# One level of Strassen's algorithm in the gate and up products of a transformer step on Trainium2

## The chip, the core and the metric

The kernel runs on one core of one Trainium2 chip, as one launch. The metric is the device time of the launch in microseconds (us). A core has the matrix engine TensorE (PE; its weight loads are shown apart as PEld), VectorE (DVE), ScalarE (ACT) and GpSimd (POOL), and a queue (SP) that issues the DMAs. Each engine works through its own list of instructions in order and waits for the others at semaphores. On-chip data lie in SBUF; PE writes its sums to PSUM, whose 2 KB rows by partition are called banks here.

## The reference, cut to what matters

The reference is one step of a two-layer diffusion backbone on 128 prompt tokens and 512 sample tokens, in float32. Each layer is a half-step SwiGLU network (FFN), a token mixing, and a second such FFN; the change is in the four FFNs.

```python
D_MODEL, D_FF, DEPTH, SEQ, DEC_SEQ = 1024, 2816, 2, 128, 512

def swiglu(h, w_gate, w_up, w_down):
    return (jax.nn.silu(h @ w_gate) * (h @ w_up)) @ w_down

def half_ffn(x, shift, scale, gate, w_gate, w_up, w_down, g, b):
    h = modulate(x, shift, scale)
    return post_norm(x, FFN_HALF * swiglu(h, w_gate, w_up, w_down), gate, g, b)
```

The nine shift, scale and gate vectors of a layer are silu(c) times a 1024 x 9216 matrix `w_ada`, once for the prompt and once for the sample. Layer 0 mixes by attention, layer 1 by a Fourier transform.

## The kernel before

Features lie on the partitions (eight tiles of 128, index k), and the 640 tokens on the free axis, in two parts of 256 and 384 columns (first FFN) or 254 and 386 (the other three). The 2816 hidden features are 22 blocks f of 128.

A float32 product is run as three products of the type float32r. Each operand is split into a high part `hi`, rounded to float32r, and the rest `lo`, and PE sums w_hi x_hi, w_hi x_lo and w_lo x_hi in one bank (`mm3`, L398). A split is a cast (ACT or DVE) and a subtraction (DVE or POOL). Every weight is read from memory once per launch and split once: `block` (L386) takes one raw tile of [128, 1024] and makes hi and lo of it, the cast and the subtraction as one instruction each.

An FFN (`ffn`, L822) goes through the f in six groups (`GROUPS`, L37). For one f it runs gate and up for both parts: 2 x 2 x 8 k x 3 = 96 products. `hidden` (L922) takes silu(gate) x up from PSUM and splits it into `hd`. After each group come the down products of its f, for both parts and eight output tiles o, and `add_out` (L546) adds each finished bank times the gate vector to `ya` on DVE, in one instruction for a part without prompt tokens and two for the part with them.

Beside that, the first three FFNs work through the `w_ada` matrix. `matvec` (L433) multiplies a loaded tile [128, 1024] with silu(c) and sums it along the free axis, on DVE, two instructions per tile for the two vectors (the trace calls them `junk<-raw,cond,bada`, each followed by a short read of the sum). These are 48, 32 and 48 tiles in the first, second and third FFN, and none in the fourth.

The order of each engine's instructions is fixed when the program is built. PE's products are emitted in line. The other engines' work is written as generators, and `tick` (L325) emits their next pieces up to `AHEAD` = 500 ns before PE's estimated time. Where a piece may go to DVE or POOL (`sums`, L186) or to ACT or DVE (`copies`, L196), `choose` (L297) gives it to the engine that is estimated to end first, DVE with a handicap of `SPARED` = 200 ns. So a wrong estimate changes the order, and an engine whose turn it is waits, with all that is queued behind it.

At the end of an FFN the last group's down sums are normalised (mean, variance, scale, split of the next input into `hh` and `hl`), which is DVE, POOL and ACT work on eight tiles of each part; the next FFN's first products need it.

Helper functions record every operation of an engine under one line: L134 for DVE, ACT and POOL, L359 for PE.

Of the kernel before, what the change touches and what calls it, by code (L numbers as in the profile page):

```python
# [36 lines left out]
GROUPS = ((0, 4), (4, 4), (8, 4), (12, 4), (16, 2), (18, 4))  # L37
# [6 lines left out]
# Of the scheduling below, in ns: how far ahead of TensorE's queue the other engines' pieces are emitted, what  # L44
# speaks against DVE where a piece can go elsewhere, and what counts as the same time.
# [9 lines left out]
def pieces(parts, t0, n):  # L55
    """Where the tokens t0 to t0 + n lie: (part, column, tokens before, tokens)."""
    out = []
    for half, runs in enumerate(parts):
        for c, t, m in runs:
            a, b = max(t, t0), min(t + m, t0 + n)  # L60
            if a < b:
                out.append((half, c + a - t, a - t0, b - a))
    return out


class Clock:
    """Estimates in ns: by tile, when it will be written (and by which engine) and when its slot is free."""

    def __init__(self):
        self.ready, self.used, self.free = {}, {}, {}  # L70


class Pool:
    """A pool of tiles that notes which tile follows which in a slot; since: when its memory is free at the earliest."""
# [15 lines left out]
    def used(self, name):  # L90
        """When the last tile of that name will be through."""
# [3 lines left out]
class Slots:  # L95
    """Tiles of one shape in a pool, taken and given back in any order."""
# [7 lines left out]
    def free(self, n):  # L104
        return len(self.rest) >= n

    def take(self, n=None):
        ts = []
        for _ in range(n or 1):
            used = lambda x: self.of[x][0].used(x)  # L110
            name = min(self.rest, key=used)
            self.rest.remove(name)
            pool, shape, dtype = self.of[name]
            ts.append(pool.tile(shape, dtype, name=name, bufs=1))
            self.names[ts[-1].tensor.name] = name
        return ts if n else ts[0]

# [5 lines left out]
class Queue:  # L123
    """An engine, with an estimate in ns of when it will be through what it has been given."""
# [12 lines left out]
    def cost(self, op, args, aps, kw):  # L137
# [12 lines left out]
    def after(self, x):  # L150
        """When tile x can be read."""
        if x.tensor.name not in self.clock.ready:
            return 0
        t, of = self.clock.ready[x.tensor.name]
        return t + ((125 if of == "v" else 0) if of == self.name else 250 if self.name == "t" else 200 if of == "t" else 130)

    def run(self, aps, outs, dur):
# [6 lines left out]
        for x in outs:  # L164
            c.ready[x.tensor.name] = self.t, self.name
        for x in (*aps, *outs):
            c.used[x.tensor.name] = max(c.used.get(x.tensor.name, 0), self.t + 200)


class Loads:  # L170
    """The DMA queue."""
# [4 lines left out]
    def dma_start(self, out, in_):  # L176
        c = self.clock
        self.issued = max(self.issued, c.free.pop(out.tensor.name, 0), c.ready.get(in_.tensor.name, (0, 0))[0]) + 50
        self.t = max(self.t, self.issued) + 4e-3 * int(np.prod(out.shape)) / 0.354
        c.ready[out.tensor.name] = self.t + 1800, "d"  # L180
        c.used[out.tensor.name] = max(c.used.get(out.tensor.name, 0), self.t + 1800)
        c.used[in_.tensor.name] = max(c.used.get(in_.tensor.name, 0), self.t + 1800)
# [1913 lines left out]
```

## Time and profile before

| | before |
|---|---|
| time, median of 3 runs | 2508.52 us (2504.37 to 2513.58) |
| span of the profiled execution | 2503.6 us |
| PE busy | 2413.5 us (96%) |
| DVE busy | 1595.8 us (64%) |
| ACT busy | 723.5 us (29%) |
| POOL busy | 641.9 us (26%) |
| DMA | 259.03 MB, mean 103 GB/s |

The span runs from the first to the last instruction of the core. No time of the profiled execution is shown but its span, which lies 4.9 us below the median of the timed runs. The first FFN's body (its groups of f, without its start and its last normalisation) lies at 112 to 365 us, the second's at 980 to 1235, the third's at 1458 to 1712, the fourth's at 2090 to 2345. In the page's 40 slices of 62.6 us each, the digit is the busy share, or for PEclk the granted clock, in tenths. A busy PE is the time from a product's start to its modelled end, and single products overlap, so their pace is read from the distance of starts, not from a product's own duration.

### The profile page before, as it was taken

The numbers are of one execution on the slowest core, as the hardware profiler recorded it, in microseconds if no ns is written. First come the engines' busy times: TensorE is split into PE (matmuls) and PEld (weight loads), VectorE is DVE, ScalarE is ACT, GpSimd is POOL, SyncE is SP. The second block draws the span as 40 slices with busy tenths as digits, with TensorE's granted clock in tenths as the row PEclk, the third lists the DMA queues.
The fourth block names the chain that finished last, engine by engine and source line by source line (L and its number), as shares of the span: only waits on it lengthen the run. The fifth ranks groups of instructions, "written<-read, shape, count | busy, mean of one in ns | idle before, by whom it ended". The sixth has DMA issues, their size and how long they took to land. (4 is left out here: it accounts for less than half of the span.)

```text
span 2503.6 us, 39511 instructions
## 1 busy us (share of the span) xinstructions
PE 2413.5 (96%) x15713; PEld 2314.1 (92%) x15713; DVE 1595.8 (64%) x3194; ACT 723.5 (29%) x1475; POOL 641.9 (26%) x499
## 2 busy tenths in 40 slices
PE   7999999989989999999999999999989989999997
PEld 7999999987577999999999999999976879999997
DVE  8867766677567686456566677676687963323346
ACT  3221212254666442112122322211234322221122
POOL 6312221242322152013112421100245522201112
PEclk8999999999899999999999999999999989999998
DMA  6535434140012225134240354443423213112121
GB/s 247 177 118 176 143 118 160 34 135 31 7 36 78 85 84 169 64 122 149 95 136 27 102 174 137 132 147 118 136 81 108 90 43 102 65 63 76 51 76 43
DMA packets 86025, 259.03 MB, mean 103 GB/s; under 512 B 13832, under 2 KB 26824, under 8 KB 85712
## 3 DMA queue, kind: packets, MB, share of 16 engines
q1 hardware_dynamic: 85840, 256.50, 31.0%
q8 instruction: 124, 2.03, 0.3%
q14 instruction: 61, 0.50, 0.1%
HBM read 248.84 MB, written 5.52 MB: 102 GB/s over the span
## 5 line engine op out<-in xcount | busy, mean ns | idle before, releaser
L359 PE MATMUL a<-hh,wu 128*128 128x254 f32 (+3 forms) x3840 | 855.1, 311 | 4.7 <-DVE hh L134 4.6
L359 PEld LDWEIGHTS a<-hh,wu 128*128 128x128 f32 x3840 | 653.4, 190 | 6.7 <-DVE hh L134 5.8
L359 PE MATMUL a<-hd,wd 128*128 128x254 f32 (+3 forms) x4224 | 629.1, 310 | 3.7 <-DVE ya L134 3.4
L359 PEld LDWEIGHTS a<-hd,wd 128*128 128x128 f32 x4224 | 624.2, 189 | 6.7 <-issue 3.7
L359 PE MATMUL a<-hl,wu 128*128 128x386 f32 (+3 forms) x1920 | 597.5, 311 | 3.0 <-POOL hl L134 1.6
L359 PE MATMUL a<-hh,w 128*128 128x254 f32 (+6 forms) x2240 | 504.2, 314 | 1.3 <-ACT hh L134 0.9
L134 DVE CUSTOM_DVE_ANT_0 junk<-raw,cond,bada 128x1024 bf16<-128x1024 f32 x256 | 379.0, 1481 | 12.3 <-DMA raw<-in_w_ada 7.8
L359 PEld LDWEIGHTS a<-hh,w 128*128 128x128 f32 (+1 forms) x2240 | 380.2, 191 | 7.1 <-issue 2.5
L359 PEld LDWEIGHTS a<-hl,wu 128*128 128x128 f32 x1920 | 364.9, 190 | 4.6 <-DVE hl L134 2.2
L134 DVE TENSOR_TENSOR tmp<-tmp,a 128x254 f32<-128x254 f32 (+3 forms) x176 | 85.5, 486 | 430.1 <-PE a L359 420.3
L359 PE MATMUL a<-hl,w 128*128 128x254 f32 (+4 forms) x1056 | 329.8, 312 | 3.0 <-POOL hl L134 2.0
L134 DVE SCALAR_TENSOR_TENSOR ya<-a,gate,ya 128x128 f32<-128x128 f32 (+3 forms) x576 | 226.7, 433 | 145.7 <-PE a L359 144.7
L134 POOL TENSOR_TENSOR wu<-raw,wu 128x1024 fp32r<-128x1024 f32 x55 | 150.4, 2744 | 633.0 <-ACT wu L134 617.0
L134 ACT CAST hd<-tmp 128x386 fp32r<-128x386 f32 (+3 forms) x163 | 75.5, 463 | 513.2 <-DVE tmp L134 513.0
L359 PEld LDWEIGHTS a<-hl,w 128*128 128x128 f32 (+1 forms) x1056 | 200.4, 190 | 6.4 <-POOL hl L134 2.8
L134 POOL TENSOR_TENSOR w<-raw,w 128x1024 fp32r<-128x1024 f32 (+3 forms) x49 | 106.9, 2189 | 357.9 <-ACT w L134 356.8
L134 ACT ACTIVATE tmp<-a 128x254 f32<-128x254 f32 (+3 forms) x176 | 76.8, 437 | 323.3 <-PE a L359 322.6
L134 ACT CAST wu<-raw 128x1024 fp32r<-128x1024 f32 x110 | 113.2, 1047 | 160.4 <-DMA raw<-in_w_gu 122.1
L134 ACT CAST wd<-raw 128x1024 fp32r<-128x1024 f32 x66 | 68.2, 1047 | 254.7 <-PE a L359 153.7
L134 DVE TENSOR_TENSOR hd<-tmp,hd 128x254 fp32r<-128x254 f32 (+3 forms) x152 | 89.3, 588 | 65.2 <-ACT hd L134 64.9
L134 POOL TENSOR_TENSOR wd<-raw,wd 128x1024 fp32r<-128x1024 f32 x22 | 60.4, 2749 | 193.7 <-ACT wd L134 150.8
L134 DVE TENSOR_TENSOR wd<-raw,wd 128x1024 fp32r<-128x1024 f32 x70 | 95.0, 1365 | 10.5 <-ACT wd L134 9.8
(438 smaller groups left out, 2575.8 us busy)
## 6 DMA issues: line engine op xcount, KB each, us to landing
raw<-in_w_gu SPq DMA_DIRECT2D x176, 512.0 KB, 3.7
raw<-in_w_ada SPq DMA_DIRECT2D x128, 512.0 KB, 3.8
raw<-in_w_dn SPq DMA_DIRECT2D x88, 512.0 KB, 3.6
raw<-in_w_fin SPq DMA_DIRECT2D x16, 520.0 KB, 3.8
wd<-in_w_ada SPq DMA_DIRECT2D x16, 512.0 KB, 7.5
raw<-in_w_ab SPq DMA_DIRECT2D x11, 512.0 KB, 3.7
raw<-in_w_abo SPq DMA_DIRECT2D x8, 512.0 KB, 4.3
raw<-in_w_fout SPq DMA_DIRECT2D x8, 512.0 KB, 3.6
```

Of the source, the lines that this page charges most:

```text
L134: return getattr(self.engine, op)(*args, **kw)
L359: pe.engine.matmul(out, w, x, **kw)
```

## The change

For f = 3 to 19 (4 to 19 in the first FFN) the gate and up products are seen as one product of 2 x 2 blocks: rows gate and up, inner index the even and the odd features, columns the first and the last 320 tokens. One level of Strassen's algorithm in Winograd's form takes seven block products in place of eight. Each is 4 k x 3 = 12 products of 320 columns, so such an f takes 84 products in place of 96. Of the 88 f of the four FFNs, 16 + 3 x 17 = 67 go this way. The plain f that are left are 0 to 2 (0 to 3 in the first FFN), 20 and 21.

What a Strassen f needs beside the products: `weights` forms S1 to S4 from the four raw blocks of [128, 512] (four sums), and `operand` splits A11, A22, S1, S2, A12, S3, S4 (seven casts and seven subtractions of 512 columns, in place of two of each of 1,024). Once per FFN `form` builds T1 to T4 from the input in four steps (16 sums of 320 columns and 16 splits). Of the block sums, U2 and U3 are used twice, so `snap` copies a bank to SBUF on ACT three times per f, and DVE adds from PSUM.

The groups become eight, of 3, 3, 3, 3, 3, 2, 2, 3 f (`FOURS` keeps the old ones in another place), so there are two more rounds of down sums per FFN. The down sums of a group now come after the first f of the next group, and a Strassen f's last two block products are held back (`pending`) until the next f has begun. The number of raw tiles goes from 3 to 4, and the estimates of DVE's and PE's instructions are altered.

```diff
-GROUPS = ((0, 4), (4, 4), (8, 4), (12, 4), (16, 2), (18, 4))
+THREES = ((0, 3), (3, 3), (6, 3), (9, 3), (12, 3), (15, 2), (17, 2), (19, 3))
+FOURS = ((0, 4), (4, 4), (8, 4), (12, 4), (16, 2), (18, 4))
+HALF = NT // 2
+EVENODD = (0, 2, 4, 6, 1, 3, 5, 7)
+PARTS = ("A11", "A22", "S1", "S2", "A12", "S3", "S4")
...
-            return (0.52 if twice else 1.04) * n + 68 + 62 * len(by)
+            return (0.52 if twice else 1.04) * n + 150 + 62 * len(by)
...
-    return {"v": 68 + 1.04 * n, "g": 150 + 2.1 * n}
+    return {"v": 150 + 1.04 * n, "g": 150 + 2.1 * n}
...
-        pe.run([w, x], [out], max(0.833 * size(w) * (2 if x.dtype == F32 else 1), (0.4167 * size(x) + 2.5) * (4 if x.dtype == F32 else 1)))
+        pe.run([w, x], [out], max(0.833 * size(w) * (2 if x.dtype == F32 else 1), (0.44 * size(x) + 7) * (4 if x.dtype == F32 else 1)))
...
+        plain = 4 if early else 3
+        fast = lambda f: plain <= f < FT - 2
...
+                if fast(f):
+                    units += [("s", 0, f)]
...
+            if g < last:
+                held = [("d", half, o, g) for half in (0, 1) for o in ([(0, 1, 2)] if half == 0 else [(0,), (1,), (2,)]) + [(o,) for o in range(3, KT)]]
...
+        def operand(f, part, src, known):
+            key = "s", f, part
+            yield None, lambda: may(key, 1, False)
+            eng = yield copies(src), src
+            yield None, lambda: may(key, 1, False)
+            tickets.popleft()
+            t = ops.take()
+            self.clock.cut(t, D // 2)
+            hi, lo = t[:, :D // 2], t[:, D // 2:]
+            copy(eng, hi, src)
+            eng = yield sums(D // 2), hi
+            eng.tensor_tensor(lo, src, hi.bitcast(F32), ALU.subtract)
+            wf[f, part] = hi, lo
+            known.add(part)
...
+        def weights(f):
+            raws, known, n = graw[f], set(), D // 2
+            halves = lambda t: (t[:, :n], t[:, n:])
+            put = lambda part, src: self.spawn(operand(f, part, src, known))
+            a11, a12 = halves(raws[0])
+            put("A11", a11)
+            yield None, lambda: 1 in raws
+            a21, a22 = halves(raws[1])
+            put("A22", a22)
+            s3, s2, s1, s4 = a21, a22, a11, a12
+            eng = yield sums(n), a21
+            eng.tensor_tensor(s3, a11, a21, ALU.subtract)
+            yield None, lambda: "A22" in known
+            eng = yield sums(n), s3
+            eng.tensor_tensor(s2, a22, s3, ALU.subtract)
+            yield None, lambda: "A11" in known
+            eng = yield sums(n), s2
+            eng.tensor_tensor(s1, s2, a11, ALU.add)
+            put("S1", s1)
+            put("S2", s2)
+            put("A12", a12)
+            yield None, lambda: "A12" in known
+            eng = yield sums(n), s2
+            eng.tensor_tensor(s4, a12, s2, ALU.subtract)
+            put("S3", s3)
+            put("S4", s4)
+            yield None, lambda: len(known) == 7
+            self.raws.give(raws[0], raws[1])
+            del graw[f]
...
+        def form(p):
+            n = HALF
+            yield None, lambda: all(h[half][k] is not None for half in range(2) for k in (2 * p, 2 * p + 1))
+            b11, b12, b21, b22 = (xs[p][:, n * k:n * k + n] for k in range(4))
+            if p + 1 < KT // 2:
+                self.spawn(form(p + 1))
+            yield None, lambda: self.tmps.free(3) and self.xt.free(1)
+            a, b = (t[:, :n] for t in self.tmps.take(2))
+            ts = [self.xt.take(dtype=F32R)]
+            self.clock.cut(ts[0], n, 2 * n, 3 * n)
+            def split(x, t, c):
+                hi, lo = t[:, c:c + n], t[:, c + n:c + 2 * n]
+                eng = yield copies(x), x
+                copy(eng, hi, x)
+                eng = yield sums(n), hi
+                eng.tensor_tensor(lo, x, hi.bitcast(F32), ALU.subtract)
+                return hi, lo
+            eng = yield sums(n), xs[p]
+            eng.tensor_tensor(a, b12, b11, ALU.subtract)
+            eng = yield sums(n), xs[p]
+            eng.tensor_tensor(b, b22, b12, ALU.subtract)
+            forms["T1", p] = yield from split(a, ts[0], 0)
+            eng = yield sums(n), b
+            eng.tensor_tensor(a, b, b11, ALU.add)
+            forms["T3", p] = yield from split(b, ts[0], 2 * n)
+            eng = yield sums(n), a
+            eng.tensor_tensor(b, b21, a, ALU.subtract)
+            self.xt.give(xs[p])
+            ts.append(self.xt.take(dtype=F32R))
+            self.clock.cut(ts[1], n, 2 * n, 3 * n)
+            forms["T2", p] = yield from split(a, ts[1], 0)
+            forms["T4", p] = yield from split(b, ts[1], 2 * n)
+            self.tmps.give(a, b)
+            formed.extend(ts)
...
+        def product(ps, f, part, xs, start):
+            self.need(lambda: (f, part) in wf)
+            w = wf.pop((f, part))
+            for k in range(KT // 2):
+                self.mm3(ps, [x[:, 128 * k:128 * k + 128] for x in w], xs(k), start and k == 0, k == KT // 2 - 1, not start)
+                if k == KT // 2 - 1:
+                    ops.give(w[0])
+                self.tick()
...
+        b11, b21, b22 = block_of(0, 0), block_of(1, 0), block_of(1, HALF)
+        t1, t2, t3, t4 = (formed_by(f"T{k}") for k in (1, 2, 3, 4))
...
+        def snap(st, name, ps):
+            yield "s", ps
+            yield "s", lambda: self.tmps.free(1)
+            st[name] = self.tmps.take()[:, :HALF]
+            nc.scalar.copy(st[name], ps)
...
+        def gate_a(f, st):
+            yield "v", st["b3"]
+            t = st["p1"]
+            yield "v", t
+            nc.vector.tensor_tensor(t, st["b3"], t, ALU.add)
+            self.banks.give(st["b3"])
+            yield "s", t
+            nc.scalar.activation(out=t, in_=t, func=AF.Silu)
+            yield "v", lambda: "up a" in st
+            yield "v", st["b1"]
+            nc.vector.tensor_tensor(t, t, st["b1"], ALU.mult)
+            self.banks.give(st["b1"])
+            yield from kept(f, "a", t, slice(0, HALF))
...
+        def up_b(st):
+            yield from snap(st, "u3", st["b1"])
+            st["u3 there"] = 1
+            t = st["u3"]
+            yield "v", t
+            nc.vector.tensor_tensor(t, st["b2"], t, ALU.add)
+            st["up b"] = 1
+        def gate_b(f, st):
+            yield "v", st["b2"]
+            t, up = st["u2"], st["u3"]
+            nc.vector.tensor_tensor(t, st["b2"], t, ALU.add)
+            self.banks.give(st["b2"])
+            yield "s", t
+            nc.scalar.activation(out=t, in_=t, func=AF.Silu)
+            eng = yield sums(HALF), t
+            eng.tensor_tensor(t, t, up, ALU.mult)
+            self.tmps.give(up)
+            yield from kept(f, "b", t, slice(HALF, NT))
...
+        def p4(f, st):
+            self.need(lambda: "u3 there" in st)
+            product(st["b1"], f, "A22", t4, False)
+            st["up a"] = 1
+        def p3(f, st):
+            self.need(lambda: "up b" in st)
+            product(st["b2"], f, "S4", b22, False)
+            self.spawn(gate_b(f, st), first=1)
...
+        def strassen(f):
+            st = {}
+            st["b1"] = self.take()[:, :HALF]
+            product(st["b1"], f, "A11", b11, True)
+            self.spawn(snap(st, "p1", st["b1"]), first=1)
+            st["b2"] = self.take()[:, :HALF]
+            product(st["b2"], f, "S1", t1, True)
+            flush(1)
+            self.need(lambda: "p1" in st)
+            product(st["b1"], f, "S2", t2, False)
+            self.spawn(snap(st, "u2", st["b1"]), first=1)
+            st["b3"] = self.take()[:, :HALF]
+            product(st["b3"], f, "A12", b21, True)
+            self.spawn(gate_a(f, st), first=1)
+            flush(1)
+            self.need(lambda: "u2" in st)
+            product(st["b1"], f, "S3", t3, False)
+            self.spawn(up_b(st), first=1)
+            pending.extend([(p4, f, st), (p3, f, st)])
...
-    g["w_gu"] = w.reshape(DEPTH, 2, 2, KT, 128, FT, 128).transpose(0, 1, 5, 2, 4, 3, 6).reshape(DEPTH, 2, FT, 2, 128, D)
+    g["w_gu"] = w.reshape(DEPTH, 2, 2, KT, 128, FT, 128)[:, :, :, EVENODD, :].transpose(0, 1, 5, 2, 4, 3, 6).reshape(DEPTH, 2, FT, 2, 128, D)
```

On DVE, in a group of the third FFN, this stood in the program before: two `w_ada` products, the splits of down weights (`wd`), and one f's hidden block (`mod` is the short read after a `w_ada` product):

```order
L134 ISA junk,mod_5_14177<-raw_15982,cond,bada 128x1024
L134 ISA mod_5_14177 128x1
L134 CAST wd<-raw_15986 128x1024
L134 TENSOR_TENSOR wd<-raw_15986,wd 128x1024
L134 TENSOR_TENSOR tmp_15998<-tmp_15998,a_15957 128x386
L134 CAST hd_5_16012<-tmp_15998 128x386
L134 TENSOR_TENSOR hd_4_16013<-tmp_15998,hd_5_16012 128x386
L134 TENSOR_TENSOR wd<-raw_15993,wd 128x1024
```

At a like place of the changed program stand the sums S1 to S4 made in place in the raw tiles, and the splits of their results into `wu` and `w`, ahead of two `w_ada` products:

```order
L183 TENSOR_TENSOR raw_16635<-raw_16635 128x512
L183 TENSOR_TENSOR raw_16633<-raw_16635,raw_16633 128x512
L183 CAST wu_16831<-raw_16635 128x512
L183 CAST w_16836<-raw_16633 128x512
L183 TENSOR_TENSOR wu_16829<-raw_16633,wu_16829 128x512
L183 TENSOR_TENSOR w_16836<-raw_16633,w_16836 128x512
L183 TENSOR_TENSOR wu_16851<-raw_16635,wu_16851 128x512
L183 ISA junk,mod_5_14549<-raw_16779,cond,bada 128x1024
L183 ISA mod_5_14549 128x1
L183 ISA junk,mod_5_14549<-raw_16779,cond,bada 128x1024
L183 ISA mod_5_14549 128x1
L183 TENSOR_TENSOR tmp_16824<-a_16861,tmp_16824 128x320
```

What moved in: the sums over halves of a raw tile, each waiting for the one before, stand ahead of the `w_ada` products and of the sum from PSUM (`tmp<-a,tmp`), which now all stand behind them in DVE's list.

On PE, at the same place, the program before went from one f's gate chain straight to its up chain, three products for each k:

```order
L359 MATMUL a_15957<-hh_7_14132,w 128x386
L359 MATMUL a_15957<-hl_7_14133,w 128x386
L359 MATMUL a_15957<-hh_7_14132,w 128x386
L359 MATMUL a_16008<-hh_0_14030,wu 128x386
L359 MATMUL a_16008<-hl_0_14031,wu 128x386
L359 MATMUL a_16008<-hh_0_14030,wu 128x386
```

Now the last k of A11 x B11 goes to one bank (`a_16804`), S1 x T1 (`xt` holds the T) to a second, and S2 x T2 is then added to the first bank:

```order
L433 MATMUL a_16804<-hh_84,w_16534 128x320
L433 MATMUL a_16804<-hl_92,w_16534 128x320
L433 MATMUL a_16804<-hh_84,w_16534 128x320
L433 MATMUL a_16820<-xt_14885,wu_16578 128x320 x3
L433 MATMUL a_16820<-xt_14912,wu_16578 128x320 x3
L433 MATMUL a_16820<-xt_14995,wu_16578 128x320 x3
L433 MATMUL a_16820<-xt_15066,wu_16578 128x320 x3
L433 MATMUL a_16804<-xt_14961,wu_16583 128x320 x3
```

What moved: between the two uses of the first bank stands ACT's copy of it (`snap`), so PE's list now waits on ACT within an f, and on each split of an operand 12 products ahead of its use, where it waited on one split for 48 products.

## Rows read from the trace of the kernel before

**Rows 1.** The page: its first line, PE's totals, the granted clock in 40 slices.

```profile
span 2503.6 us, 39511 instructions
PE 2413.5 (96%) x15713; PEld 2314.1 (92%) x15713; DVE 1595.8 (64%) x3194; ACT 723.5 (29%) x1475; POOL 641.9 (26%) x499
...
PEclk8999999999899999999999999999999989999998
```

**Rows 2.** Busy us (x instructions), clock, DMA by stretch; columns named first.

```profile
core 0: us, PE busy (x) PEld busy (x) DVE busy (x) ACT busy (x) POOL busy (x), PEclk, DMA share, GB/s
112.00:365.00 253.00, 253.00 (x1728) 253.00 (x1728) 175.18 (x264) 51.34 (x78) 57.61 (x21) 1.00 0.41 138
1458.00:1712.00 254.00, 254.00 (x1726) 254.00 (x1725) 181.43 (x289) 52.38 (x77) 36.89 (x14) 1.00 0.45 148
2090.00:2345.00 255.00, 255.00 (x1736) 255.00 (x1734) 80.78 (x149) 51.10 (x76) 36.16 (x13) 1.00 0.22 72
...
1847.00:2090.00 243.00, 212.96 (x1183) 185.51 (x1182) 178.25 (x423) 86.00 (x212) 112.59 (x97) 0.91 0.29 95
...
1373.00:1458.00 85.00, 81.80 (x528) 81.07 (x529) 62.15 (x116) 31.07 (x59) 41.75 (x35) 0.98 0.32 107
```

**Rows 3.** Timeline of PE in the second FFN: start us, us, instruction.

```profile
1300.35 0.34 PE L359 MATMUL a<-hl,wu 128*128 128x386 f32 x1
...
1300.88 0.34 PE L359 MATMUL a<-hl,wu 128*128 128x386 f32 x1
```

**Rows 4.** Third FFN, 1458 to 1712: groups on DVE; count, busy us, mean ns, idle before.

```profile
L134 DVE CUSTOM_DVE_ANT_0 junk<-raw,cond,bada 128x1024 bf16<-128x1024 f32 x70 | 103.0, 1472 | 2.1 <-DMA raw<-in_w_ada 1.1
...
L134 DVE SCALAR_TENSOR_TENSOR ya<-a,gate,ya 128x386 f32<-128x386 f32 x24 | 14.6, 617 | 5.4 <-PE a L359 5.4
...
L134 DVE SCALAR_TENSOR_TENSOR ya<-a,gate,ya 128x128 f32<-128x128 f32 x24 | 8.3, 344 | 2.1 <-PE a L359 2.1
...
L134 DVE TENSOR_TENSOR tmp<-tmp,a 128x386 f32<-128x386 f32 x12 | 6.7, 557 | 31.0 <-PE a L359 31.0
...
L134 DVE DVE_READ_ACCUMULATOR2_ANT mod<- 128x1 f32 x70 | 5.7, 82 | 0.0
...
L134 DVE TENSOR_TENSOR hd<-tmp,hd 128x386 fp32r<-128x386 f32 x10 | 5.6, 562 | 5.3 <-ACT hd L134 5.2
```

**Rows 5.** Fourth FFN, 2090 to 2345: groups on DVE.

```profile
L134 DVE TENSOR_TENSOR wu<-raw,wu 128x1024 fp32r<-128x1024 f32 x8 | 9.8, 1219 | 4.2 <-ACT wu L134 4.2
...
L134 DVE TENSOR_TENSOR tmp<-tmp,a 128x254 f32<-128x254 f32 x12 | 5.0, 420 | 36.8 <-PE a L359 36.8
...
L134 DVE CAST wd<-raw 128x1024 fp32r<-128x1024 f32 x3 | 2.1, 695 | 7.1 <-DMA raw<-in_w_dn 7.1
...
L134 DVE CAST hd<-tmp 128x254 fp32r<-128x254 f32 x3 | 0.9, 295 | 0.1
```

**Rows 6.** First FFN, 112 to 365: groups on DVE.

```profile
L134 DVE CUSTOM_DVE_ANT_0 junk<-raw,cond,bada 128x1024 bf16<-128x1024 f32 x63 | 99.1, 1574 | 2.1 <-DMA raw<-in_w_ada 1.2
...
L134 DVE TENSOR_TENSOR hd<-tmp,hd 128x256 fp32r<-128x256 f32 x12 | 11.7, 974 | 4.3 <-ACT hd L134 4.3
...
L134 DVE CAST wd<-raw 128x1024 fp32r<-128x1024 f32 x4 | 4.5, 1123 | 1.7 <-DMA raw<-in_w_dn 1.7
```

**Rows 7.** Whole run: groups on POOL.

```profile
L134 POOL TENSOR_TENSOR w<-raw 128x512 f32<-128x512 f32 x8 | 10.0, 1275 | 0.0
...
L134 POOL TENSOR_TENSOR w<-raw,w 128x384 fp32r<-128x384 f32 x6 | 6.0, 1003 | 34.9 <-ACT w L134 34.9
```

**Rows 8.** All products of junk: minimum, median, maximum ns.

```profile
L134 DVE CUSTOM_DVE_ANT_0 junk<-raw,cond,bada x256: 1271/1285/3368, 75.3 to 1788.1; 128x1024 bf16<-128x1024 f32 x128
```

**Rows 9.** Timeline of POOL from 264 us: start, us, instruction, wait before it.

```profile
264.12 2.39 POOL L134 TENSOR_TENSOR wu<-raw,wu 128x1024 fp32r<-128x1024 f32 x1 [31.40 <-ACT wu L134]
```

**Rows 10.** Timeline of DVE over the same 2.4 us.

```profile
264.25 0.62 DVE L134 SCALAR_TENSOR_TENSOR ya<-a,gate,ya 128x384 f32<-128x384 f32 x1 [0.71 <-PE a L359]
264.79 2.80 DVE L134 CUSTOM_DVE_ANT_0 junk<-raw,cond,bada 128x1024 bf16<-128x1024 f32 x1
```

More of the change, by code (lines that the diff above doesn't have):

```diff
@@ L814, in start, with first_blocks, ffn @@
         self.spawn(rest())
-    def gu_block(self, l, j, n, pool, dst, turn=0):
-        own = (self.wp, "w", 4) if (n + turn) % 6 < 2 else (pool, "wu", 8)
-        return self.io["w_gu"][l, j, n // 2, n % 2], self.block(dst, n, *own)
-    def ffn(self, l, j, i, nxt, pool, gu, first, turn=0, ada=0, urgent=0, after=(), early=False, **kw):
+    def first_blocks(self, l, j, dst, ops, m, only=None):
+        place, when = lambda: ops.take(only=only), lambda: ops.free(2, only)
+        return [(self.io["w_gu"][l, j, n // 2, n % 2], self.block(dst, n, place, when)) for n in range(m)]
+    def ffn(self, l, j, i, nxt, pool, ops, gu, first, groups, ada=0, urgent=0, after=(), early=False, reserve=True, **kw):
         nc, io = self.nc, self.io
@@ L916, in head, with through, hid_of, kept @@
                 for b in range(2):
-                    self.mm3(pair[b], [x[:, kt * 128:kt * 128 + 128] for x in gu[2 * f + b]], h[half][kt],
+                    self.mm3(pair[b], [x[:, k:k + 128] for x in gu[2 * f + b]], h[half][kt],
                              kt == 0 and not (one and b), kt == KT - 1 and not (one and not b))
             left[0] -= 1
+            through(half, 2 * f, 2 * f + 1)
             self.spawn(hidden(f, half, *pair))
+        read = {}
+        def through(half, *ns):
+            for n in ns:
+                read.setdefault(n, set()).add(half)
+                if len(read[n]) == 2:
+                    back(*gu[n])
+        def hid_of(f):
+            if f not in hid:
+                hid[f] = hids.take(2)
+                for t in hid[f]:
+                    self.clock.cut(t, 254, 256, HALF)
+            return hid[f]
+        def kept(f, key, t, c):
+            n = c.stop - c.start
+            room = lambda: f in hid or hids.free(2)
+            yield None, room
+            eng = yield copies(t), t
+            yield None, room
+            hi, lo = (x[:, c] for x in hid_of(f))
+            copy(eng, hi, t)
+            eng = yield sums(n), hi
+            eng.tensor_tensor(lo, t, hi.bitcast(F32), ALU.subtract)
+            self.tmps.give(t)
+            hidden_by.add((f, key))
         def hidden(f, half, pg, pu):
@@ L932, in hidden @@
             self.banks.give(pu)
-            yield None, lambda: hids[half].free(2)
-            eng = yield copies(t), t
-            yield None, lambda: hids[half].free(2)
-            hi, lo = (x[:, :self.n[half]] for x in hids[half].take(2))
-            copy(eng, hi, t)
-            eng = yield sums(size(hi)), hi
-            eng.tensor_tensor(lo, t, hi.bitcast(F32), ALU.subtract)
-            self.tmps.give(t)
-            hid[f, half] = hi, lo
+            yield from kept(f, half, t, self.cols(half))
@@ new lines, in ffn, with flush @@
+        pending = []
+        def p4(f, st):
[6 more added lines that the diff above has]
+            self.spawn(gate_b(f, st), first=1)
+        def flush(n=2):
+            while pending and n:
+                fn, *args = pending.pop(0)
+                fn(*args)
+                n -= 1
+            if formed and not pending and here[0] >= end_t:
+                self.xt.give(*formed)
+                formed.clear()
@@ L943, in out, with hidden_there @@
+        def hidden_there(f, half):
+            if not fast(f):
+                return (f, half) in hidden_by
+            return (f, "a") in hidden_by and (half == 0 or (f, "b") in hidden_by)
         def out(half, o, ps, g):
@@ L1597, in ab_out @@
         done = [-1]
-        loads = [(None, io["w_abo"][o], self.block(w, o, pool, *(("wu", 8) if o < 4 else ("wd", 8)))) for o in range(KT) if o not in w]
+        took = [t for t in w]
+        room = lambda: ops.free(2) or self.xt.free(6)
+        place = lambda: ops.take() if ops.free(1) else self.xt.take(dtype=F32R)
+        loads = [(None, io["w_abo"][o], self.block(w, o, place, room)) for o in range(KT) if o not in w]
         loads += [(lambda n=n: done[0] >= max(n, 1), *x) for n, x in enumerate(nxt)]
```

410 lines of the change are left out of this document (289 added, 121 removed).

## The prediction, made before the changed kernel ran

> **What bounds the kernel now.** I read the page first, then the windows of the FFN bodies, then the groups of instructions in them. PE is busy for 2413.5 of 2503.6 us, with the granted clock at its upper level (1.00, 2.4 GHz) nearly everywhere [rows 1]. In the bodies of the first, third and fourth FFN the windows show PE busy for every microsecond at 1.00 [rows 2]: the order of the other engines doesn't matter there yet, and a product saved is time saved. The same windows show who is next. DVE is busy 181.4 of 254 us in the third FFN, 175.2 of 253 in the first, but 80.8 of 255 in the fourth, which has no `w_ada` work [rows 2]. So PE gets shorter exactly where DVE has some 30% left in two FFNs, and plenty in the fourth.
>
> **What the change removes.** PE's pace: 254 us for 1726 products is 0.147 us each [rows 2], over equal numbers of 254 and 386 columns, a mean of 320. That it goes by columns is seen in the timeline: three products of 386 take 1300.88 - 1300.35 = 0.53 us, 0.177 each [rows 3], against 0.147 x 386/320 = 0.177. So a product of 320 columns is 0.147, and a Strassen f takes 84 x 0.1472 = 12.36 us in place of 96 x 0.1472 = 14.13. That is 1.77 us for each of 67 f, 118.3 us, as long as PE isn't kept waiting. From the profiled span that leaves 2385.3, or 2390 in terms of the median, which stands 4.9 us above that span.
>
> **What it adds on PE's path.** The bank of A11 x B11 is reused after ACT's copy. Between them stand 12 products, 1.77 us; ACT is busy 52 of 254 us [rows 2], and even twice that per f leaves it half idle, so I cost the copies at nothing. If ACT is late, that is up to some 0.5 us for each of three copies (DVE's sum of 386 columns from PSUM takes 0.557 [rows 4]), 67 x 1.5 = 100 us at the very most.
>
> **What it adds on DVE and POOL.** I count one full group of three f in the third FFN, from the new order, by rows of before. PE: 3 x 12.36 + 144 down products x 0.147 = 58.3 us. DVE:
> - 8 output tiles x (0.617 + 2 x 0.344) [rows 4] = 10.4;
> - 16 `w_ada` products of 1.285 undisturbed [rows 8] + 0.082 for the read [rows 4] = 21.9;
> - 12 sums of 320 columns from PSUM, between 0.420 at 254 [rows 5] and 0.557 at 386 [rows 4], so 0.489 = 5.9;
> - subtractions from SBUF: 0.562 at 386 [rows 4] and 1.219 at 1,024 [rows 5] are 1.03 ns a column, so 4 of 320 at 0.49, 15 of 512 at 0.69 and 3 of 1,024 at 1.22 = 16.1;
> - 5 casts of 512 at 0.43 (between 0.295 at 254 and 0.695 at 1,024 [rows 5]) and one of 0.695 = 2.8.
>
> That is 57.1 us beside PE's 58.3: it would just fit. POOL gets 18 subtractions of 512 at 1.275 and 5 of 320 at 0.87 (from 1.003 at 384 and 1.275 at 512) [rows 7] = 27.3 us, so POOL itself is far from full. Counted alike, the other groups of the third FFN are (PE / DVE / POOL) 58.3/54.0/29.4 for the first, 45.9/43.5/20.9 and 26.5/27.3/14.9 for the short ones and 67.7/53/19.5 for the last; the three in the middle average 56.6 and 27.1. The first FFN is like it but for its first group (43.2 on DVE). The second's groups have 38 to 51 on DVE, the fourth's 38.
>
> **The open price is what POOL takes from DVE.** In the timeline a POOL subtraction runs from 264.12 for 2.39 us, to 266.51 [rows 9]. A DVE sum from PSUM that begins at 264.25 takes its 0.62 as ever; the `w_ada` product after it, begun at 264.79, takes 2.80 in place of 1.285 and ends 1.08 after POOL [rows 8, 10]. It did its work when POOL was through.
>
> The Trainium skill, "SBUF — State Buffer", section "SBUF: two separate sides", says that the two engines' shared port pair is an exclusive lock, held for a whole instruction by whichever came first, and not a shared bandwidth. The trace agrees (the 2.80 us above). By that rule alone no DVE operation with two SBUF inputs could lie beside POOL, and the sum would be that of the slower case below.
>
> How much DVE loses for each us of POOL is read from sums. In the third FFN 70 products of mean 1.472 lost 70 x 0.187 = 13.1 us to 36.9 us of POOL, 0.36 [rows 2, 4, 8]; in the first 63 x 0.289 = 18.2 to 57.6, 0.32 [rows 2, 6]. With the first FFN's other groups (12 x (0.974 - 0.42), 4 x (1.123 - 0.695) [rows 5, 6]) it is 26.5 to 57.6, 0.46. In the fourth the subtraction of 1,024 stays at 1.219 [rows 5], no loss seen. So the price lies between 0 and 0.46, above it only if a full DVE meets POOL more often; I take 1/3, near the two FFNs that have `w_ada` work.
>
> **The sum.** A middle group then takes DVE 56.6 + 27.1/3 = 65.6 us, 7.3 over PE's 58.3, and more than the 63.6 that three f took before. Third FFN: 5.5 + 3 x 7.3 + 4.6 + 5.8 = 38 us of waits, the last group being bound by PE. First: 31, by the same steps, its first group having room. Second: 7, nearly all in the short groups. Fourth: none. Sum 76.
>
> The starts of the FFNs come on top: the T blocks are made while the normalisation runs. Around the third's start, DVE is busy 62 and POOL 42 of 85 us before [rows 2]; the new order has, from the second's last down sums to the first Strassen f, 148 instructions on DVE, some 62 us by the durations above, and 58 on POOL, some 52, so 62 + 52/3 = 79 beside PE's 64 and the 3 us that it waited there before [rows 2]: +12. For the other three I take a little over a third of that each, since there the work has more PE time beside it: 25 in all, between 0 and 40.
>
> The granted clock fell to 0.91 where PE was busy 213 of 243 us [rows 2]. The waits above are 11% of a group's time, so it could fall in the new groups too. But 58.3/0.91 = 64 is still under 65.6: where DVE is the bound, a slower PE costs nothing more. I take 0, with 25 as the other end.
>
> Sum: 2503.6 - 118.3 + 76 + 25 = 2486, as a median 2491 us. DVE becomes the bound in two FFNs, and most of what PE saves is waited away.
>
> **Rivals.**
> B, the gain stays: POOL runs mostly beside DVE's sums from PSUM (16.3 of the 57.1 us) and in DVE's gaps, at a price of 0.1, nearer the fourth FFN's. A middle group is 59.3, 1.0 over PE; the waits come to 11, the starts to 10: 2503.6 - 118.3 + 21 + 4.9 = 2411. For it: DVE's undisturbed work fits. Against it: the two FFNs in question showed three times that price with a third less work on DVE.
>
> C, slower: DVE pays 0.46, as the first FFN did over all its groups, because it hardly has a gap left in which POOL could run. A middle group is 56.6 + 0.46 x 27.1 = 69.1, 10.8 over; third FFN 56, first 46, second 18, starts 30: 150 us of waits, and 2503.6 - 118.3 + 150 + 4.9 = 2540. It decides from a price of 0.38, where waits and saving are equal. For it: the subtractions that were one instruction of 1,024 are two of 512 and more of them, so DVE meets POOL more often. Against it: POOL is stretched as well when it comes second, and then DVE pays nothing.
>
> **Chances.** A (2491) 0.42, its own range 2460 to 2515; B (2411) 0.26, 2395 to 2455; C (2540) 0.32, 2515 to 2590. 0.5% is 12.5 us, about what a measurement can tell from no change here, so "same" is 2496 to 2521. A gives 0.19 faster, 0.19 same, 0.04 slower; B 0.26 faster; C 0.02 same, 0.30 slower. That makes 0.45, 0.21 and 0.34. The range of 2412 to 2562 leaves out the lower half of B and the worst of C, some 0.2.
>
> **What would show it.** Right: in the bodies of the first and third FFN, DVE above 90% and PE near 88%, with PE's waits ended by DVE or POOL splits (`wu`, `w`); `w_ada` products of mean 1.5 us and more; a full group every 65 us there, and 58.3 in the fourth FFN, whose body is 17 x 1.77 = 30 us shorter. Wrong for B: the third FFN's group at 59 us with PE full. Wrong for C: 69 us or more. Wrong altogether: PE waiting for ACT's copies or for banks, in the fourth FFN too, or a product of 320 columns off 0.147.

## The result, and the profile after

The changed kernel takes 2671.93 us (median of 4 runs, 2668.3 to 2681.27) against 2511.05 for the kernel before beside it: ratio 1.0652, interval 1.0626 to 1.0679. The forecast was 2491 us, in a range of 2412 to 2562. The change is slower by 161 us, beyond the slower rival C (2540) too.

The page of the changed kernel, its first line, the totals and the granted clock [rows 1 before]:

```profile
span 2666.4 us, 39992 instructions
PE 2378.4 (89%) x14909; PEld 2249.9 (84%) x14909; DVE 2117.0 (79%) x3917; ACT 900.0 (34%) x1976; POOL 1257.2 (47%) x999
...
PEclk7999999999899998999999999999997999999998
```

PE lost time in two ways. It idles 2666.4 - 2378.4 = 288 us where it idled 90, and it is busy 83 us more than the 2413.5 - 118.3 = 2295 that the smaller number of products should take. Together that is 281 us: the 118 that were saved and the 163 that the span grew. By stretches, in us, cut at the starts of products in PE's timeline (saved: 1.77 us for each Strassen f):

| stretch, to | before | after | saved | lost |
|---|---|---|---|---|
| first FFN's last down product | 505.6 | 555.8 | 28.3 | 78.5 |
| last attention score | 330.5 | 348.7 | 0 | 18.2 |
| third FFN's last down product | 1016.1 | 1113.1 | 60.2 | 157.2 |
| last Fourier output product | 139.3 | 139.3 | 0 | 0 |
| fourth FFN's last down product | 493.4 | 486.1 | 30.1 | 22.8 |
| end | 18.7 | 23.4 | 0 | 4.7 |

The windows of the first FFN, two middle groups of the third and two of the fourth, and the start [rows 2]; the groups of DVE and POOL in the third FFN's window [rows 4 and 7]:

```profile
core 0: us, PE busy (x) PEld busy (x) DVE busy (x) ACT busy (x) POOL busy (x), PEclk, DMA share, GB/s
125.00:479.00 354.00, 315.49 (x2046) 310.56 (x2047) 311.41 (x495) 98.22 (x195) 183.35 (x120) 0.97 0.39 124
1646.00:1786.00 140.00, 123.71 (x792) 121.91 (x792) 123.47 (x194) 39.13 (x80) 69.52 (x46) 0.95 0.42 128
2301.00:2424.00 123.00, 118.48 (x787) 117.47 (x788) 87.05 (x145) 35.54 (x70) 52.52 (x36) 0.99 0.26 78
...
0.00:125.00 125.00, 94.22 (x550) 91.52 (x550) 106.39 (x138) 39.30 (x77) 83.36 (x65) 0.82 0.53 187
```

```profile
L183 DVE CUSTOM_DVE_ANT_0 junk<-raw,cond,bada 128x1024 bf16<-128x1024 f32 x32 | 50.2, 1570 | 1.2 <-DMA raw<-in_w_ada 0.9
L183 DVE TENSOR_TENSOR wu<-raw,wu 128x512 fp32r<-128x512 f32 x16 | 14.4, 910 | 0.4 <-ACT wu L183 0.4
...
L183 DVE TENSOR_TENSOR raw<-raw,raw 128x512 f32<-128x512 f32 x8 | 8.8, 1095 | 4.0 <-POOL wu L183 2.7 <-POOL w L183 1.2
L183 DVE TENSOR_TENSOR tmp<-a,tmp 128x320 f32<-128x320 f32 x18 | 8.5, 479 | 0.1
...
L183 POOL TENSOR_TENSOR wu<-raw,wu 128x512 fp32r<-128x512 f32 x17 | 24.6, 1458 | 6.8 <-DVE wu L183 3.9 <-ACT wu L183 2.9
```

A middle group of the third FFN takes 140/2 = 70 us, of the fourth 61.5, where PE needs 58.3. In the third, DVE is busy for 123.5 of the 140 us, PE for 123.7, ACT for 39: no engine is full. DVE's sums from PSUM keep the counted time (0.479 us, counted 0.489); its operations from SBUF are stretched, 0.69 to 0.91 and 1.10, and POOL's of 512 columns from 1.275 to 1.458.

PE's waits in the whole run (us, times, longest) name neither DVE nor POOL first:

```profile
PE a L433 <- ACT tmp L183: 134.2, 59, 7.7
PE a L433 <- DVE ya L183: 23.7, 20, 2.0
```

`ACT tmp` is `snap`, the copy of a bank. One such wait in the timelines of PE, ACT, DVE and POOL:

```profile
1681.86 0.31 PE L433 MATMUL a<-hh,w 128*128 128x320 f32 x1
1686.68 3.25 PE L433 MATMUL a<-xt,wu 128*128 128x320 f32 x12 [4.51 <-ACT tmp L183]
1689.73 0.47 PE L433 MATMUL a<-hh,w 128*128 128x320 f32 x1
...
1685.68 0.62 ACT L183 CAST wu<-raw 128x512 fp32r<-128x512 f32 x1 [2.09 <-DVE raw L183]
1686.21 0.42 ACT L183 COPY tmp<-a 128x320 f32<-128x320 f32 x1
...
1683.87 1.73 DVE L183 TENSOR_TENSOR raw<-raw,raw 128x512 f32<-128x512 f32 x1 [0.77 <-POOL wu L183]
1685.52 0.48 DVE L183 TENSOR_TENSOR hd<-tmp,hd 128x320 fp32r<-128x320 f32 x1
1685.92 0.68 DVE L183 CAST wu<-raw 128x1024 fp32r<-128x1024 f32 x1
...
1682.11 2.94 POOL L183 TENSOR_TENSOR wu<-raw,wu 128x512 fp32r<-128x512 f32 x2
```

Read it from the bottom up. POOL runs two splits from 1682.11. DVE's sum for an operand waits for the first and then, beside the second, takes 1.73 us. ACT's cast of that operand waits 2.09 us for the sum. The copy that PE wants could have run before 1685.68, but stands behind that cast in ACT's list. PE, through at 1682.2, waits 4.51 us, and its next 12 products take 1689.73 - 1686.68 = 3.05 us, 0.254 each in place of 0.147. It is no rare case: in 42 of the 59 waits, some 128 of the 134 us, ACT itself had stood waiting, mostly for a result of DVE or POOL, at an instruction that lies ahead of the copy and ended after PE had stopped. The windows after and before the wait shown (in this order) have the granted clock at 0.61 after it, a mix of its two levels, and at 1.00 before it:

```profile
1686.60:1691.00 4.40, 4.32 (x19) 4.32 (x20) 4.40 (x8) 2.03 (x5) 0.03 (x1) 0.61 0.79 238
1677.00:1682.00 5.00, 5.00 (x36) 4.91 (x34) 4.77 (x5) 2.06 (x4) 4.19 (x3) 1.00 0.12 30
```

### The profile page after: what moved, and what is told of

Read it like the earlier page. It is cut to its first block, busy times and chain, and to the rows that moved or that the text cites. A ratio compares the mean times of both kernels' runs of the same rounds, so it can differ in the third digit from the quotient of the medians.

```text
span 2666.4 us, 39992 instructions
## 1 busy us (share of the span) xinstructions
PE 2378.4 (89%) x14909; PEld 2249.9 (84%) x14909; DVE 2117.0 (79%) x3917; ACT 900.0 (34%) x1976; POOL 1257.2 (47%) x999
## 5 line engine op out<-in xcount | busy, mean ns | idle before, releaser
L433 PE MATMUL a<-hh,wu 128*128 128x320 f32 (+4 forms) x2320 | 562.1, 317 | 17.5 <-ACT hh L183 12.0
L433 PE MATMUL a<-hd,wu 128*128 128x254 f32 (+3 forms) x2784 | 525.4, 313 | 30.4 <-DVE ya L183 23.7
L433 PE MATMUL a<-xt,wu 128*128 128x320 f32 (+2 forms) x2372 | 400.8, 324 | 89.9 <-ACT tmp L183 89.6
L433 PEld LDWEIGHTS a<-hd,wu 128*128 128x128 f32 x2784 | 443.8, 191 | 35.9 <-issue 22.8
L433 PEld LDWEIGHTS a<-xt,wu 128*128 128x128 f32 x2372 | 371.1, 198 | 105.0 <-ACT tmp L183 103.0
L183 POOL TENSOR_TENSOR wu<-raw,wu 128x512 fp32r<-128x512 f32 (+1 forms) x198 | 331.9, 1683 | 229.2 <-PE a L433 77.2
L433 PEld LDWEIGHTS a<-hh,wu 128*128 128x128 f32 x2320 | 411.8, 194 | 21.5 <-ACT hh L183 13.1
L433 PE MATMUL a<-hl,wu 128*128 128x320 f32 (+4 forms) x1168 | 369.3, 316 | 4.6 <-DVE hl L183 3.3
L433 PE MATMUL a<-hd,w 128*128 128x254 f32 (+3 forms) x1232 | 278.0, 311 | 0.0
L433 PE MATMUL a<-hh,w 128*128 128x320 f32 (+6 forms) x1048 | 265.8, 321 | 4.9 <-ACT hh L183 3.9
```

Of the source, the lines that this page charges most:

```text
L183: return getattr(self.engine, op)(*args, **kw)
L433: pe.engine.matmul(out, w, x, **kw)
```

## The experiments

**The price of POOL by itself** (`port`).

> Not the model: a kernel that only runs DVE and POOL instructions on constant data, in eleven stretches set apart by a common wait, and writes zeros. Alone: 24 DVE differences of 512 columns from SBUF, 24 DVE sums of 320 from PSUM, 24 DVE casts of 512, 12 products like those with w_ada, 24 POOL differences of 512. Then together with 24 POOL differences (30.6 us): 48 DVE differences (33 us alone), 64 PSUM sums (31), 64 casts (28), 24 products (32), and two mixes. Theory (a DVE operation that reads only SBUF and a POOL one exclude each other): the stretch of the differences takes nearly the sum, 55 to 64 us, the products' too, that of the PSUM sums nearly the longer one, 31 to 40. Rival (they share a bandwidth, or DVE pays a third): 33 to 45 us for each of them.

```diff
+    phases = [((two,), 24, 0), ((psum,), 24, 0), ((cast,), 24, 0), ((product,), 12, 0), ((), 0, 24),
+              ((two,), 48, 24), ((psum,), 64, 24), ((cast,), 64, 24), ((product,), 24, 24),
+              ((psum, two), 24, 24), ((psum, psum, two, product, two, psum, two, product), 6, 24)]
```

The timeline, alone and then together with 24 POOL operations:

```profile
9.16 17.41 DVE L2094 TENSOR_TENSOR vo<-va,vb 128x512 f32<-128x512 f32 x24
27.23 12.56 DVE L2100 TENSOR_TENSOR vo<-a,va 128x320 f32<-128x320 f32 x24
40.43 11.04 DVE L2097 COPY vo<-va 128x512 f32<-128x512 f32 x24
...
68.72 32.08 POOL L2106 TENSOR_TENSOR go<-ga,gb 128x512 f32<-128x512 f32 x24 [0.27 <-DVE vo L2091]
...
101.51 57.42 DVE L2094 TENSOR_TENSOR vo<-va,vb 128x512 f32<-128x512 f32 x48
159.59 33.56 DVE L2100 TENSOR_TENSOR vo<-a,va 128x320 f32<-128x320 f32 x64
193.73 52.02 DVE L2097 COPY vo<-va 128x512 f32<-128x512 f32 x64
```

Alone, 24 operations of a kind were run (12 products); the times alone below are scaled to the number run together. 48 differences take 57.4 us where they take 34.8 alone: POOL's 32.1 us cost DVE 22.6, a price of 0.70 (us of DVE for each us of POOL). The casts pay 0.70 too (52.0 for 29.4), the products like those with `w_ada` 0.63 (51.9 for 31.8), the sums from PSUM nothing (33.56 for 33.5). A mix nearer a group's (three of eight operations from PSUM) took 51.8 for 38.4, a price of 0.42; where every second one is from PSUM it was 40.5 for 30.0, 0.33. So the theory holds for the differences and the sums from PSUM; the products lie between the two expectations. The Trainium skill ("SBUF — State Buffer", section "SBUF: two separate sides") calls the two engines' shared port pair an exclusive lock for the whole instruction. By that rule alone the differences would take the strict sum, 34.8 + 32.1 = 66.9, an estimate; measured are 9.5 us less, 0.4 per POOL operation, so the trace agrees for the most part and not wholly.

**Less work on DVE** (`narrow_ada`).

> The changed program in the same order, with each w_ada product on 64 of its 1,024 columns (15/16 of that sum is left out). Theory (DVE and POOL together are the bound): DVE loses about 19 us a group in the first and third FFN, whose groups fall from 69 to the fourth's 61 to 63 us, the second's from 67 to 62; in all 80 to 110 us less, 2560 to 2590. Rival (PE waits for ACT's copies because of the order, not the load): groups stay within 2 us of 69, the time at 2650 or more.

```diff
-            out=self.junk, in0=w, in1=self.cond[:, v], scale=1.0, scalar=b,
...
+        q, n, acc = self.nc.vector, 64, out[:, o, v:v + 1]
...
+            out=self.junk[:, :n], in0=w[:, :n], in1=self.cond[:, v, :n], scale=1.0, scalar=b,
```

2578.27 us, 94 less, as the theory said in sum. By groups (timed from one round of down products to the next) it was only half right: 63 to 68 us in the first and third FFN, not 61 to 63, with DVE busy for 87.6 of 131 us:

```profile
180.00:311.00 131.00, 121.23 (x795) 119.74 (x794) 87.58 (x194) 38.89 (x78) 60.91 (x47) 0.97 0.42 137
```

PE still waited 91.4 us for ACT's copies. So DVE's load is not all: with a third of its time free, results that ACT's list stands waiting for still come late.

**ACT's list** (`narrow_cast`).

> As narrow_ada (each w_ada product on 64 of 1,024 columns, the rest of that sum left out), and the casts of S1 to S4 given to DVE, never to ACT. Theory (ACT's copies of a bank stand in its list behind casts that wait for DVE's and POOL's sums, and PE waits for the copy): PE's waits for ACT copies fall by half or more, and the groups of the first and third FFN go from 65 to 66 down to 59 to 62, the whole to 2530 to 2560. Rival (the load on DVE and POOL alone): DVE has 5 us a group more to do, so groups of 65 or more and 2575 or more.

```diff
-            eng = yield copies(src), src
+            eng = yield {"v": copies(src)["v"]} if part[0] == "S" else copies(src), src
```

2558.28 us, 20 less than `narrow_ada` although DVE has more to do; groups of 60.5 to 64.6, where 59 to 62 were expected. The direction is the theory's, but the waits for ACT fell only from 91.4 to 76.2 us, not by half. These four casts are one part of what ACT's copies stand behind (first line `narrow_ada`, second `narrow_cast`):

```profile
PE a L433 <- ACT tmp L183: 91.4, 41, 5.9
PE a L433 <- ACT tmp L183: 76.2, 47, 7.2
```

**POOL barred** (`no_pool`).

> The changed program with POOL barred from the sums and differences of the FFNs: DVE does them all, some 15 us more a group by undisturbed durations. Theory (POOL's operations shut DVE out): a middle group of the first and third FFN takes 57 + 15 = 72 us, 2 to 5 more than the 68.7 now, the fourth FFN's groups (38 + 13 = 51 on DVE) come to PE's 58.3 to 60; in all 2640 to 2700. Rival (POOL's work lies beside DVE's and takes little from it; PE waits for other reasons): 15 us a group more in the first and third FFN, 2800 and over.

```diff
 def sums(n):
+    if NOPOOL[0]:
+        return {"v": 150 + 1.04 * n}
```

`NOPOOL[0]` is set while an FFN is emitted. 2641.91 us, 30 less. The fourth FFN's groups come to 58.3 us, as expected. In the third they are 65 to 71, not 72. In the first they are 58.3, which I had not expected: the planner, with DVE estimated full, put some 7 `w_ada` products in a group and not 16, and ran the rest after the FFN, where from its last down product to the last score 420 us passed and not 349 (45 of them in one wait of PE for a DMA). With all 67 f, DVE's work doesn't fit beside PE's either way; barring POOL moves it behind the FFN.

**What isn't Strassen** (`no_strassen`, `old_estimates`, `no_strassen_old`, `before_new_estimates`).

> The changed program with no Strassen f in any FFN: all 22 f are plain, the T blocks aren't built; its slots, groups of three, layout and altered estimates stay. Theory (the work that Strassen adds on DVE and POOL is what costs): that work is gone, a group of three f takes PE's 63.6 us again, and the time is 2511 within 20 us. Rival (the altered estimates and slots make a bad order): the stretch from the first FFN's last down product to the last attention score stays at 349 us (330 before), and the whole at 2550 or more.

> The changed program with the planner's old estimates (DVE 68 ns and not 150 an instruction, PE 0.4167 n + 2.5). Theory (load, not order): within 20 us of 2672. Rival (the estimates spoil the order): 2620 or less, with attention back at 330 us.

> no_strassen with the planner's old estimates. Theory (of the 37 us that no_strassen stands above the kernel before, the estimates make most, in the attention): 2510 to 2525, the attention stretch at 335. Rival (slots and layout make them): 2535 or more.

> The kernel before with the change's estimates (DVE 150 ns and not 68 an instruction in the planner, PE 0.44 n + 7), nothing else. Theory (the estimates by themselves cost 15 us, as between no_strassen and no_strassen_old): 2520 to 2535. Rival (they only matter beside the new slots): 2512 within 8.

```diff
+FAST = ()
...
-        fast = lambda f: plain <= f < FT - 2
+        fast = lambda f: (l, j) in FAST and plain <= f < FT - 2
```
```diff
-            return (0.52 if twice else 1.04) * n + 150 + 62 * len(by)
+            return (0.52 if twice else 1.04) * n + 68 + 62 * len(by)
```

`no_strassen` takes 2544.99 us (ratio 1.0133, 1.0097 to 1.017): groups are back at 63.5, but the stretch to the last score is at 358, and the total lies between both expectations. `old_estimates` takes 2641.29, 31 less than the changed kernel, between both expectations too. `no_strassen_old` takes 2530.22 (1.0066, 1.0045 to 1.0087), between both expectations again. The kernel before with the new estimates takes 2537.8 (1.0108, 1.0091 to 1.0126), 29 more, about half of it in the attention (346.8 us for 330.5). So the altered estimates cost some 15 to 31 us in these three pairs, slots, layout and groups 17 to 22, and Strassen itself, under the old estimates, 2641 - 2530 = 111. I had given neither of the first two a term.

**How much Strassen, and with POOL or not.** Three runs first:

> Strassen f only in the fourth FFN, which has no w_ada work; the other three are plain as in no_strassen. Theory: DVE has room there, so of the 30 us that PE saves some are kept; the fourth FFN takes 486 us from the Fourier output to its last down product as in the changed kernel, and the time is 5 to 15 us below no_strassen. Rival (Strassen loses wherever it is, by its order on PE and ACT): no faster than no_strassen.

> The changed program with POOL barred only from the splits and sums of weights, operands and hidden blocks; the T blocks and the normalisations keep it. Theory (DVE loses about two thirds of each POOL operation, so POOL gives DVE nothing): groups of the fourth FFN at 58.3, PE's pace, in place of 61 to 62.6, and its stretch from the Fourier output to the last down product 10 to 15 us shorter than the changed kernel's 486; the first and third FFN stay bound by DVE with 16 w_ada products a group (or leave such products for their end); 2590 to 2640 in all. Rival (POOL helps): fourth FFN unchanged or longer, 2670 and over.

> Strassen f in the fourth FFN alone, POOL barred from the splits and sums of weights, operands and hidden blocks in all four, old estimates. Theory: no_strassen_old (2530) less 15 to 25 us of the fourth FFN: 2505 to 2515. Rival: the fourth FFN gains nothing, 2530.

`last_ffn_only` takes 2547.16 us, no faster than `no_strassen` (2544.99): groups gain 2.3 us each (61.2 for 63.5), the start of that FFN and its last groups give it back. So far the rival. `body_no_pool` has the fourth FFN's groups at 58.4, but takes 2660.38 us, more than expected: that FFN is 4 us shorter, not 10 to 15, since PE now waits 22.9 us in one piece at its start for a weight split (`wu`) on DVE, and `w_ada` products are put off as in `no_pool`. With POOL barred (`alone` offers DVE only) and old estimates, `last_no_pool` takes 2505.34 (0.9974, 0.9956 to 0.9991), as expected.

```diff
-            eng = yield sums(D // 2), hi
+            eng = yield alone(D // 2), hi
```

Then fewer Strassen f, spread over the first three FFNs, with more of the `w_ada` products put beside the plain f (the last two lines of the cut):

> As body_no_pool, with as many Strassen f as DVE has room for, spread evenly: 10, 14, 10 and 17 of the 22 f in the four FFNs (51 in place of 67), and more w_ada work put beside the plain f. Theory (DVE's own sum is what counts): the FFN bodies run at PE's pace, 51 x 1.77 = 90 us less than no_strassen, of which the T blocks at the starts take back 20 to 40: 2475 to 2500. Rival (the order within a Strassen f costs, not the load): waits for ACT's copies stay at 100 us or more in all, 2540 and over.

> half_new with the planner's old estimates, which took 15 us from no_strassen. Theory: 2460 to 2490, below the kernel before. Rival: as half_new, 2525 and over.

> half_old with POOL allowed in the FFN bodies as in the changed kernel: 51 Strassen f, old estimates. Theory (POOL's operations take from DVE about two thirds of their length): DVE falls behind in the first three FFNs, groups of 61 to 64 us in place of 58 to 62, and the time 20 to 50 us above half_old's 2500. Rival (fewer Strassen f were all that mattered): 2500 or less.

> body_no_pool with the old estimates: all 67 Strassen f, no POOL in the bodies. Theory (in the first and third FFN DVE's own sum, 72 us a group, is over PE's 58): well above half_old, 2560 to 2630, with w_ada products left over to the FFNs' ends or groups of 65 to 71. Rival (POOL was the only trouble): 2500 or less.

```diff
+FAST = {(0, 0): (4, 6, 8, 9, 11, 12, 14, 16, 17, 19), (0, 1): (3, 4, 6, 7, 8, 9, 10, 12, 13, 14, 15, 16, 18, 19), (1, 0): (3, 5, 7, 8, 10, 12, 14, 15, 17, 19), (1, 1): (3, 4, 5, 6, 7, 8, 9, 10, 11, 12, 13, 14, 15, 16, 17, 18, 19)}
...
+        fast = lambda f: f in FAST[l, j]
...
-            clock += (begins[t + 1] - begins[t]) * {"gk": 0, "g": 1, "s": 1, "d": 2}[u[0]]
+            clock += (begins[t + 1] - begins[t]) * {"gk": 0, "g": 2, "s": 0.5, "d": 2}[u[0]]
```

| time in us, old estimates | POOL in the bodies | none |
|---|---|---|
| 67 Strassen f | 2641.29 | 2631.05 |
| 51 Strassen f | 2591.31 | 2499.73 |

PE's waits for ACT's copies in these four runs, by rows (67 f with POOL, without; 51 f with POOL, without):

```profile
PE a L433 <- ACT tmp L183: 116.6, 54, 12.3
PE a L437 <- ACT tmp L183: 13.6, 13, 8.9
PE a L434 <- ACT tmp L184: 78.7, 37, 12.3
PE a L438 <- ACT tmp L184: 11.7, 7, 8.9
```

Neither edit is enough alone (the rows differ in the place of the `w_ada` products too); both together take 142 us off. With 51 f, POOL costs 92 us, more than the 20 to 50 expected, and 67 us of the waits for ACT's copies come and go with it: the copies are the same, what changes is who makes the sums that ACT's list waits for. With 67 f it makes only 10 in the total, but not because the groups stay long. Without POOL they take 58.1 to 59.5 us in all four FFNs, PE's pace; DVE's remaining work is put off instead, 34 of the `w_ada` products to the time after the third FFN (none before), where PE waits 87.1 us in one piece. These are the windows of middle groups in the first and third FFN of `all_no_pool_old`, and of the time after the third:

```profile
169.00:365.00 196.00, 195.71 (x1332) 195.43 (x1331) 180.41 (x353) 66.47 (x128) 0.00 (x0) 1.00 0.36 116
1573.00:1790.00 217.00, 216.14 (x1467) 215.59 (x1467) 200.91 (x386) 75.68 (x146) 0.00 (x0) 1.00 0.36 118
1905.00:2012.00 107.00, 3.47 (x9) 1.92 (x8) 54.68 (x111) 8.58 (x21) 17.16 (x18) 0.52 0.23 74
```

`half_old` (2499.73; ratio 0.9959, 0.9939 to 0.9978) is below the kernel before, but missed its 2460 to 2490. `half_new` (2568.8) missed its 2475 to 2500: the new estimates take 69 us here. `all_no_pool_old` (2631.05) ended just above its 2560 to 2630. No run separates how POOL delays ACT's list: by shutting DVE out, or by its own pace (1.34 us a difference in `port`, DVE 0.73) in a chain of sums each of which waits for the one before.

Last, the largest wait left in `half_old`, 16.45 us for one split behind the T blocks:

> half_old, with POOL allowed again for the splits of the first weight blocks of each FFN (four or five of 1,024 columns in all). In half_old one of them stood on DVE behind the T blocks' sums, and PE waited 16.45 us for it at the start of the fourth FFN. Theory (a wait for a piece that stands behind other work in DVE's list): that wait goes, 2478 to 2492. Rival (something else is late there next): 2495 or more.

```diff
-                eng = yield alone(D), hi
+                eng = yield sums(D) if kind == "gu" and f < 8 else alone(D), hi
```

2489.3 us, ratio 0.9919 (0.9904 to 0.9934): the best version, 19 us below the 2508.38 of the kernel before in the same runs, with 16 Strassen f fewer than the change. Its windows of two groups in the first, third and fourth FFN:

```profile
181.00:300.00 119.00, 119.00 (x811) 118.64 (x810) 106.11 (x196) 38.27 (x69) 0.00 (x0) 1.00 0.44 142
1551.00:1671.00 120.00, 120.00 (x817) 119.83 (x817) 108.85 (x199) 37.97 (x69) 0.00 (x0) 1.00 0.45 148
2171.00:2288.00 117.00, 117.00 (x795) 116.66 (x794) 89.53 (x177) 39.38 (x77) 0.00 (x0) 1.00 0.26 82
```

PE is full at 1.00, and the fourth FFN's stretch is 465.3 us against 493.4: 28 of the 30 us saved are kept.

## Why the prediction was wrong

**PE's pace and saving: right.** A product of 320 columns takes 0.147 us, and where nothing waits a group of three f takes 58.3 to 58.4 us (fourth FFN of `half_start`).

**The mis-sized term: POOL's price.** "I take 1/3, near the two FFNs that have `w_ada` work". Those FFNs had DVE idle for 30% of the time [rows 2], so part of POOL's work probably fell into gaps. Beside a DVE that is always busy it is 0.63 to 0.70 for operations from SBUF and 0.33 to 0.42 for mixes. With 0.42 a middle group is 56.6 + 0.42 x 27.1 = 68.0; measured are 66.1 to 68.9 in the first and 68.6 to 70.5 in the third FFN, about rival C's group (69.1). That the two meet is partly luck. The sum adds durations, and one DVE instruction often starts before the last has ended (1685.52 + 0.48 against 1685.92 above): in the third FFN before, the durations add up to 195.8 us where DVE is busy for 181.4. In a middle group after they come to 67.5, but DVE is busy for only 61.5, and it idles some 7 to 9 us, about half of that waiting for POOL. So DVE wasn't full, as A and C had it, and its sum alone doesn't explain the group.

**The step that failed: ACT's copies.** "I cost the copies at nothing", because ACT is busy for only a fifth of the time. What counts is what stands ahead of a copy in ACT's list: casts that wait for DVE's and POOL's sums. 134 us of PE's waits end at these copies, and they appear in the second and fourth FFN too (62 to 68 and 61 to 63 us a group for PE's 58.3), for which I had 7 us and none. With POOL out of the FFN bodies and the old estimates they are 12 to 14 us. The prediction's bound of 100 us took a late ACT for a slow one. I had named such waits in the fourth FFN as what would show the forecast wrong altogether.

**The clock.** "I take 0, with 25 as the other end": PE was busy 83 us more than the smaller number of products should take. By the granted clock, 212 us of PE's busy time lie at 1.2 GHz, 87 in the kernel before; half of the difference, some 63 of the 83 us, is the clock's, and the rest isn't separated. In the FFN bodies every stretch at 1.2 GHz comes after a wait of PE, of 1.9 to 7.7 us, as above. This falls on PE's path because the waits come in one piece: right behind the one shown PE is busy for 4.32 of 4.40 us and is the bound.

**The starts.** 25 us expected. The stretch to the first FFN's first down product alone grew from 93 to 110 us, with PE at 94 of 125 us busy and the clock at 0.82. There the other runs separate it: 92.9 us without Strassen under the old estimates and 94.7 under the new, 106.5 with Strassen and the old. So 14 to 16 us are Strassen's (T blocks and first operands) and 2 to 4 the estimates'. With the `w_ada` products cut short (`narrow_ada`) it is 90.6: what counts is their sum on DVE. For the other starts I can't separate the two fully.

**Left out: the estimates and slots.** I read the altered constants as part of the diff and gave them no price outside the FFNs. They cost 32 to 53 us together.

## What to carry to other kernels

Before work is given to POOL, count DVE's SBUF operations and POOL's together for the busiest stage, not from an average price in a stage with gaps: beside a full DVE (`port`) a POOL difference of 512 columns cost DVE 0.94 us, more than the 0.73 that DVE needs to do it itself. An engine at 30% is no free cover for a copy that PE waits for; ask what stands ahead of the copy in that engine's list and for whom that waits. And a trade of PE time for vector work pays only while the vector engine's whole work fits: with POOL barred it did here at 51 of 88 f and didn't at 67; nothing between was run.

## What the runs showed of the hardware that was not expected

DVE's casts, which read one operand, pay the same price as the differences, which read two (0.70). A `w_ada` product cut to 64 columns still took 0.51 us on average in place of the 1.62 of the full one in the changed kernel, though its median is 0.28; that POOL stretches the others is likely but not shown. After a PE wait of 4.51 us the next 12 products ran at 0.254 us each, and 4 us later again at 0.147.
